# S5 set-up and mixing weights of a hybrid encoder layer: fewer transposes, lag zero by DMA, products by turns over strips, row sums by VectorE

## The chip, the cores and the metric

The kernel runs on one core of one Trainium2 chip. The time is device microseconds of one execution; the median of several executions is what is compared, lower is better.

The names used below: PE is TensorE's matmul side and PEld its weight load, DVE is VectorE, ACT is ScalarE, POOL is GpSimd, SP is the engine that issues most DMAs. PSUM is the memory that TensorE writes and ScalarE and VectorE read.

## The reference, cut to what matters

One layer on 512 positions of width 1024: an input projection, two mixers in parallel, a gated merge, cross-attention to 256 memory rows, and a SwiGLU feed-forward. The change touches the set-up of the two mixers.

```
def s5_scan(u, lam_re, lam_im, log_step, b_re, b_im, c_re, c_im, reverse):
    ...
    lam_bar = jnp.exp(lam * step)
    b_bar = ((lam_bar - 1.0) / lam)[..., None] * b
    bu = jnp.einsum('gpc,lbgc->lbgp', b_bar, u.astype(jnp.complex64))
    _, states = lax.associative_scan(_linear_recurrence, (a, bu), axis=0, reverse=reverse)
    return jnp.einsum('gcp,lbgp->lbgc', c, states).real

def sgu_branch(zu, zv, ln_g, ln_b, w_s, bias):
    zu = jax.nn.gelu(zu)
    zv = layer_norm(jax.nn.gelu(zv), ln_g, ln_b)
    zv = zv.reshape(bsz, seq // CHUNK, CHUNK, SGU_HEADS, SGU_HEAD_DIM)
    sv = jnp.einsum('hts,bnshd->bnthd', w_s, zv) + bias.T[None, None, :, :, None]
    return zu * sv.reshape(bsz, seq, SGU_WIDTH)
```

The S5 mixer has 32 groups of 16 channels with 64 complex states each, and runs in both directions with separate parameters (so every one of b_re, b_im, c_re, c_im has a leading axis of two directions). The gating mixer (SGU) has 8 heads, each with a 128 x 128 matrix over the positions of a chunk of 128.

## The kernel before

**Main stream.** Every large product is done in float32 precision from two parts: a weight block is loaded (`wraw`, three buffers), ScalarE casts its upper part (`whi`, line 85), VectorE subtracts to get the lower part (`wlo`, line 86), and PE adds three products of the parts (`mm3`, line 350). `plan` lists all weight blocks in order; `next_w` begins loads three blocks ahead and splits two blocks ahead. A block of 24 matmuls is a "tick" of about 5 us. The stages in order: projection to zv (first half), to the S5 input u, to zv (second half), to the gates, then the SGU mixing (`psv`), zu, the second gates with w_proj_b, the S5 output's GLU, merge, attention, feed-forward. Products go into five main PSUM banks (`bank`), side work into three (`aux`).

**Side work.** `s5_program` is a generator that hands out VectorE work between ticks; `later(n, f)` traces f n ticks later. What is traced is ordered for each engine by a scheduler that models the times beforehand; the order on each engine is then fixed in the program, and `in_order` keeps an instruction behind what was traced before it on its engine. Each engine and each DMA queue (SP's, POOL's) runs its list in order: an entry that waits holds up all behind it.

**S5 set-up** (`s5_setup`, from line 595). b_re, b_im, c_re and c_im are loaded one after another into one buffer (tag `u`) with the 32 groups on partitions (lines 625 and 630), turned by 16 transposes each (line 634, PSUM tile `pbc`, 32 rows in, 128 states of both directions out) and copied by ScalarE (line 636). VectorE makes powers of the discrete eigenvalues and b_bar.

**Kernel products** (`s5_kernels`, once for each of four octants of 8 groups). For chunks of 8 positions the response at lags -7 to 7 is made as a product: `e` (VectorE: c times powers) against `bd`, which holds b_bar of the two directions side by side in 32 columns. PSUM tile `pk` has four strips of 32 partitions, one for each group of four; `tile_position=(0, 32 * j)` puts the weights into column strip j of the array. A group takes two matmuls of 128 columns (real and imaginary part, line 786) and two of 16 columns (line 789), which add the second direction's lag zero to the first direction's. Each float32 matmul is two records of the profile. All four of a group come one after another, then the next strip's. ScalarE copies the result to `ks` (line 799), VectorE adds the skip d (line 800), POOL's queue writes it to DRAM (`spill`, eight DMAs, lines 807 and 808) and two ticks later loads it back as the Toeplitz block `tt` (`load`, line 815). `s5_outputs` uses tt in `py` (line 894). Octants 0 and 1 are made before the S5 inputs, octants 2 and 3 behind the outputs of octants 0 and 1.

**SGU weights** (`mixing_setup`, traced five ticks into the gate stage). `wsr` holds the eight mixing matrices; PE turns them (`pws`, line 998) and the layer norm's gain and offset (`pgb`, line 1001). With the offset folded out of the einsum, `mix` must hold bias + offset times the row sum of the mixing matrix: two matmuls with a matrix of ones give the row sums on every partition (`prs`, line 1007), and VectorE folds them into `mix`, into which the bias had been loaded at the start (line 1010). `psv` and the operation that adds mix (line 1035) come after the gate stage.

**Others on POOL's queue:** `pow` for the norms' roots (`r`, lines 483 and 984), small memsets, and accumulating DMAs of `plan_sums` (line 268) which add up blocks of later weights in DRAM (`qsum`, `dsum`); each waits for the plain copy that SP issues before it (line 267).

Of the kernel before, what the change touches and what calls it, by code (L numbers as in the profile page):

```python
# [9 lines left out]
F32 = mybir.dt.float32  # L10
F32R = mybir.dt.float32r
AF = mybir.ActivationFunctionType
ALU = mybir.AluOpType
AX = mybir.AxisListType
# [3 lines left out]
P = 128  # L18
# [8 lines left out]
G = 32  # L27
C = 16
GW = 1024
H = 8  # L30
# [9 lines left out]
Q = 8  # L40
# [12 lines left out]
def hybrid_layer_kernel(  # L53
# [8 lines left out]
    nc = tc.nc  # L62
# [17 lines left out]
    def aux(name, shape=(P, 512)):  # L80
        return pa.tile(list(shape), F32, tag="aux", name=name)
# [350 lines left out]
    def later(n, fn):  # L432

        side["later"].append((side["now"] + n, fn))
# [163 lines left out]
    def s5_setup():  # L598
# [19 lines left out]
            lam.append(l)  # L618
        lr, li = lam
        yield 0.3  # L620
        bc = []
        for nm, src in (("br", s5_b_re), ("bi", s5_b_im), ("cr", s5_c_re), ("ci", s5_c_im)):
            if nm[0] == "b":
                row = s5p.tile([G, 2, 64, C], F32, tag="u", name="row" + nm)
                nc.sync.dma_start(row, src[0].rearrange("d g p c -> g d p c"))
                rows = row.rearrange("g d p c -> g (d p) c")
            else:
                row = s5p.tile([G, C, 2, 64], F32, tag="u", name="row" + nm)
                for d in range(2):
                    nc.sync.dma_start(row[:, :, d, :], src[0, d])  # L630
                rows = row.rearrange("g c d p -> g (d p) c")
            ps = aux("pbc", (P, C, G))
            for c in range(C):
                nc.tensor.transpose(ps[:, c, :], rows[:, :, c], ident[:G, :G])
            t = s5p.tile([P, G, C], F32, name="raw_" + nm)
            A_.copy(t, ps.rearrange("p c g -> p g c"))
            bc.append(t)
            yield 0.1
        br, bi, cr, ci = bc
        st["c"] = (cr, ci)  # L640

# [105 lines left out]
    def lc(t, g):  # L747
        return t[:, g].rearrange("p a b -> p (a b)")
# [4 lines left out]
    def s5_kernels(o):  # L753
# [18 lines left out]
        def products():  # L772
            bd = []
            for i in range(2):
                t = s5p.tile([P, GO, 2, C], F32, tag="bd", name="bd", bufs=2)
                nc.gpsimd.memset(t, 0.0)
                for d in range(2):
                    hf = slice(64 * d, 64 * d + 64)
                    nc.scalar.copy(t[hf, :, d, :], st["b"][i][hf, gs, :])
                bd.append(t)  # L780
            ps = aux("pk", (P, 2, P))
            for q in range(2):
                for j in range(4):
                    g = 4 * q + j
                    for i in range(2):
                        nc.tensor.matmul(ps[32 * j:32 * j + 32, q, :], bd[i][:, g].rearrange("p d c -> p (d c)"),  # L786
                                         lc(es[i], g), start=(i == 0), stop=False, tile_position=(0, 32 * j))
                    for i in range(2):
                        nc.tensor.matmul(ps[32 * j:32 * j + C, q, 0:C], bd[i][:, g, 1, :],
                                         es[i][:, g, Q - 1, :], start=False, stop=(i == 1),  # L790
                                         tile_position=(0, 32 * j))
            later(1, lambda: store(ps))

        def store(ps):
# [8 lines left out]
        def spill(ks):  # L803
            kd = dp.tile([GO, C, 15, C], F32, name=f"kd{o}")
            for j in range(4):
                kdj = kd.rearrange("(q j) c l e -> j c q (l e)", j=4)[j]
                nc.gpsimd.dma_start(kdj[:, :, 7 * C:15 * C], ks[32 * j:32 * j + C])
                nc.gpsimd.dma_start(kdj[:, :, 0:7 * C], ks[32 * j + C:32 * j + 2 * C, :, 0:7 * C])
            later(2, lambda: load(kd))

        def load(kd):
# [177 lines left out]
    nc.sync.dma_start(gbr[0:H, :], sgu_ln_g[0].rearrange("(h d) -> h d", d=P))  # L989
    nc.sync.dma_start(gbr[H:2 * H, :], sgu_ln_b[0].rearrange("(h d) -> h d", d=P))  # L990
    mix = np_.tile([P, H, P], F32, tag="gain", name="mix", bufs=2)
    nc.sync.dma_start(mix, sgu_bias[0].rearrange("h t -> (h t)").partition_broadcast(P))

    def mixing_setup():
        for q in range(2):
            ps = aux("pws", (P, 4, P))
            for j in range(4):
                nc.tensor.transpose(ps[:, j, :], wsr[:, 4 * q + j, :], ident)
            nc.scalar.copy(wst[:, 4 * q:4 * q + 4, :], ps)
        ps = aux("pgb", (P, 2 * H))  # L1000
        nc.tensor.transpose(ps, gbr, ident[:2 * H, :2 * H])
        gbc = np_.tile([P, 2 * H], F32, tag="gbc", name="gbc", bufs=1)
        nc.vector.tensor_copy(gbc, ps)

        for q in range(2):
            ps = aux("prs", (P, 4, P))
            nc.tensor.matmul(ps, ones, wst[:, 4 * q:4 * q + 4, :], start=True, stop=True)
            for j in range(4):
                h_ = 4 * q + j
                nc.vector.scalar_tensor_tensor(mix[:, h_, :], ps[:, j, :], gbc[:, H + h_:H + h_ + 1], mix[:, h_, :],  # L1010
                                               ALU.mult, ALU.add)
        return gbc

    gad = dp.tile([KD, P, T], F32, name="gad")
# [4 lines left out]
        nc.sync.dma_start(gad[m - OFF_GA // P], z)  # L1019

    gbcs = []
    later(5, lambda: gbcs.append(mixing_setup()))
    for i in range(NT):
        later(1 + i, lambda i=i: layer_norm(i))
# [652 lines left out]
```

## Time and profile before

| | |
|---|---|
| median of 3 runs | 914.95 us (914.04 to 915.56) |
| span of the profiled execution | 915.4 us |
| PE busy | 900.7 us (98%) |
| DVE busy | 623.8 us (68%) |
| ACT busy | 475.4 us (52%) |
| POOL busy | 102.1 us (11%) |
| granted TensorE clock | 0.998 of full speed |

The span runs from the first to the last instruction of one execution taken by the profiler; the page gives no other time for that execution, so the runs' median stands beside the span. Busy shares are means over the whole span: a stage can be held by an engine that is idle elsewhere. A matmul's duration in the rows is its way through the array and overlaps with the next one's, so the cost of a group of matmuls is read from the distance between starts, or from the start of what follows. "Chain" is the chain of work that ended last, followed back from the last instruction.

### The profile page before, as it was taken

The numbers are of one execution on the slowest core, as the hardware profiler recorded it, in microseconds if no ns is written. First come the engines' busy times: TensorE is split into PE (matmuls) and PEld (weight loads), VectorE is DVE, ScalarE is ACT, GpSimd is POOL, SyncE is SP. The second block draws the span as 40 slices with busy tenths as digits, with TensorE's granted clock in tenths as the row PEclk, the third lists the DMA queues.
The fourth block names the chain that finished last, engine by engine and source line by source line (L and its number), as shares of the span: only waits on it lengthen the run. The fifth ranks groups of instructions, "written<-read, shape, count | busy, mean of one in ns | idle before, by whom it ended". The sixth has DMA issues, their size and how long they took to land.

```text
span 915.4 us, 14510 instructions
## 1 busy us (share of the span) xinstructions
PE 900.7 (98%) x5650; PEld 796.5 (87%) x5650; DVE 623.8 (68%) x1018; ACT 475.4 (52%) x696; POOL 102.1 (11%) x161
## 2 busy tenths in 40 slices
PE   9999999999999999999999999999999999999996
PEld 6888888888888887789899878999999999988885
DVE  5696662888753236858956836776778767899875
ACT  5542985144364334447655634745455454655664
POOL 1004420110025200101000001100020100000000
PEclk9999999999999999999999999999999999999999
DMA  8456574685546577863578416526788873246672
GB/s 252 148 148 185 124 181 141 174 193 149 153 134 146 127 219 206 275 198 120 175 216 252 139 47 184 161 88 149 189 202 212 221 186 93 69 138 200 191 244 90
DMA packets 111974, 153.80 MB, mean 168 GB/s; under 512 B 13521, under 2 KB 78561, under 8 KB 111842
## 3 DMA queue, kind: packets, MB, share of 16 engines
q1 hardware_dynamic: 93026, 128.27, 44.1%
q0 software_dynamic: 16288, 23.57, 15.9%
q10 hardware_dynamic: 2592, 1.05, 0.5%
q8 instruction: 44, 0.72, 0.3%
q14 instruction: 24, 0.20, 0.1%
HBM read 146.08 MB, written 38.24 MB: 201 GB/s over the span
## 4 chain that ended last, share of the span: by engine, by line
PE 90%; ACT 4%; DVE 3%; issue 1%; POOL 0%; DMA 0%; POOLq 0%; SPq 0%; DVEq 0%; ACTq 0%
PE pf L350 27%; PE pt L350 16%; PE px L1273 12%; PE pq L1273 6%; PE dx L350 6%; PE dq L350 3%; PE pv L1273 3%; PE qx L1273 2%; PE dv L350 2%; PE pk L786 2%; PE ptr L506 1%; PE qq L1273 1%; DVE wlo L86 1%; PE po L350 1%; ACT whi L85 1%
## 5 line engine op out<-in xcount | busy, mean ns | idle before, releaser
L86 DVE TENSOR_TENSOR wlo<-wraw,whi 128x1024 fp32r<-128x1024 f32 (+1 forms) x139 | 164.9, 1187 | 109.5 <-ACT whi L85 107.8
L85 ACT CAST whi<-wraw 128x1024 fp32r<-128x1024 f32 (+1 forms) x139 | 142.2, 1024 | 163.0 <-PE pf L350 67.0
L350 PE MATMUL pf<-xn,whi 128*128 128x512 f32 x448 | 140.1, 392 | 0.0
L350 PEld LDWEIGHTS pf<-xn,whi 128*128 128x128 f32 x448 | 83.5, 188 | 17.0 <-issue 0.2
L350 PE MATMUL pf<-xn,wlo 128*128 128x512 f32 x224 | 87.4, 390 | 0.0
L1273 PE MATMUL px<-fn,whi 128*128 128x256 f32 x480 | 86.2, 281 | 0.0
L1273 PEld LDWEIGHTS px<-fn,whi 128*128 128x128 f32 x480 | 73.4, 188 | 0.3 <-ACT u L1532 0.2
L86 DVE TENSOR_TENSOR wlo<-b,whi 128x1024 fp32r<-128x1024 f32 x40 | 48.9, 1222 | 32.8 <-ACT whi L85 32.8
L85 ACT CAST whi<-b 128x1024 fp32r<-128x1024 f32 x40 | 42.0, 1051 | 56.2 <-PE px L1273 28.9
L1273 PE MATMUL px<-fn,wlo 128*128 128x256 f32 x240 | 67.5, 281 | 0.0
L1273 PE MATMUL pq<-s,whi 128*128 128x256 f32 x320 | 57.0, 281 | 0.0
L350 PE MATMUL dx<-whi,s 128*128 128x512 f32 x170 | 53.8, 391 | 1.4 <-ACT whi L85 1.0
L86 DVE TENSOR_TENSOR wlo<-t,whi 128x1024 fp32r<-128x1024 f32 x30 | 36.7, 1224 | 20.9 <-ACT whi L85 20.9
L85 ACT CAST whi<-t 128x1024 fp32r<-128x1024 f32 x30 | 31.5, 1051 | 36.8 <-PE pv L1273 13.3
L350 PEld LDWEIGHTS pf<-xn,wlo 128*128 128x128 f32 x224 | 42.1, 188 | 8.7
L1273 PEld LDWEIGHTS pq<-s,whi 128*128 128x128 f32 x320 | 48.9, 188 | 0.1
L1273 PEld LDWEIGHTS px<-fn,wlo 128*128 128x128 f32 x240 | 46.0, 192 | 0.0
L1273 PE MATMUL pq<-s,wlo 128*128 128x256 f32 x160 | 45.0, 281 | 0.0
L350 PE MATMUL pt<-whi,xn 128*128 128x512 f32 x128 | 42.6, 405 | 0.0
L350 PEld LDWEIGHTS dx<-whi,s 128*128 128x128 f32 x170 | 31.7, 188 | 8.3 <-ACT whi L85 1.2
L350 PE MATMUL dx<-wlo,s 128*128 128x512 f32 x85 | 33.2, 391 | 0.4 <-DVE wlo L86 0.4
L1273 PEld LDWEIGHTS pq<-s,wlo 128*128 128x128 f32 x160 | 30.7, 192 | 0.0
(414 smaller groups left out, 2235.4 us busy)
## 6 DMA issues: line engine op xcount, KB each, us to landing
wraw<-in_w_in_dram SPq DMA_DIRECT2D x36, 512.0 KB, 3.8
dsum<-in_w_down_dram SPq DMA_DIRECT2D x20, 512.0 KB, 6.7
wraw<-dsum SPq DMA_DIRECT2D x20, 512.0 KB, 4.4
b<-in_w_gate_dram SPq DMA_DIRECT2D x15, 512.0 KB, 4.6
b<-in_w_up_dram SPq DMA_DIRECT2D x15, 512.0 KB, 4.6
wraw<-in_w_down_dram SPq DMA_DIRECT2D x15, 512.0 KB, 3.7
dsum<-in_w_down_dram POOLq DMA_DIRECT2D x10, 512.0 KB, 6.8
dsum<-dsum POOLq DMA_DIRECT2D x10, 512.0 KB, 7.4
```

Source lines behind the costliest of these rows:

```text
L85: hi = nc.scalar.copy(dst_hi, src)
L86: lo = nc.vector.tensor_tensor(dst_lo, src, dst_hi.bitcast(F32), ALU.subtract)
L350: nc.tensor.matmul(ps, a[x], b[y], start=start and i == 0, stop=stop and i == 2, skip_group_check=free)
L506: nc.tensor.transpose(ps[:, j, :], src[:, k * P:(k + 1) * P], ident)
L786: nc.tensor.matmul(ps[32 * j:32 * j + 32, q, :], bd[i][:, g].rearrange("p d c -> p (d c)"), lc(es[i], g), start=(i == 0), stop=False, tile ...
L1273: nc.tensor.matmul(ps[:, j, :], a[x], b[y], start=start and j == k == i == 0, stop=k == 3 and i == 2, skip_group_check=True)
```

## The change

It has five parts.

- b is loaded with real and imaginary part on 64 partitions and turned by 16 transposes for both; c is loaded with group and channel on 128 partitions and turned by 8 full transposes. Together 24 in place of 64.
- The two short matmuls of a group, which added the second direction's lag zero, are gone. The spill writes the first direction's part and the second direction's other lags as before, and four more DMAs of POOL's queue add the lag-zero block in DRAM.
- The remaining matmuls of an octant go round the four strips: first the real parts of four groups, then the imaginary parts, and so on. They are kept in program order, and the accumulation flags are set so that the first one of a strip clears it.
- The row sums of the mixing matrices come from one VectorE reduction over `wsr`, one transpose, a store to DRAM and a load that spreads them over all partitions.
- `mixing_setup` scales them by the offset (eight VectorE operations), and a DMA of POOL's queue adds the bias.

```diff
--- before.py
+++ after.py
@@ -618,24 +618,31 @@
             lam.append(l)
         lr, li = lam
         yield 0.3
-        bc = []
-        for nm, src in (("br", s5_b_re), ("bi", s5_b_im), ("cr", s5_c_re), ("ci", s5_c_im)):
-            if nm[0] == "b":
-                row = s5p.tile([G, 2, 64, C], F32, tag="u", name="row" + nm)
-                nc.sync.dma_start(row, src[0].rearrange("d g p c -> g d p c"))
-                rows = row.rearrange("g d p c -> g (d p) c")
-            else:
-                row = s5p.tile([G, C, 2, 64], F32, tag="u", name="row" + nm)
-                for d in range(2):
-                    nc.sync.dma_start(row[:, :, d, :], src[0, d])
-                rows = row.rearrange("g c d p -> g (d p) c")
-            ps = aux("pbc", (P, C, G))
-            for c in range(C):
-                nc.tensor.transpose(ps[:, c, :], rows[:, :, c], ident[:G, :G])
-            t = s5p.tile([P, G, C], F32, name="raw_" + nm)
-            A_.copy(t, ps.rearrange("p c g -> p g c"))
-            bc.append(t)
-            yield 0.1
+        raw_b = s5p.tile([P, 2, G, C], F32, name="raw_b")
+        raw_c = s5p.tile([P, 2, G, C], F32, name="raw_c")
+        brow = s5p.tile([2 * G, 2, 64, C], F32, tag="u", name="brow")
+        for i, src in enumerate((s5_b_re, s5_b_im)):
+            nc.sync.dma_start(brow[i * G:(i + 1) * G], src[0].rearrange("d g p c -> g d p c"))
+        rows = brow.rearrange("g d p c -> g (d p) c")
+        for q in range(2):
+            ps = aux("pbc", (P, C // 2, 2, G))
+            for c in range(C // 2):
+                nc.tensor.transpose(ps[:, c].rearrange("p i g -> p (i g)"), rows[:, :, q * C // 2 + c],
+                                    ident[:2 * G, :2 * G])
+            for i in range(2):
+                A_.copy(raw_b[:, i, :, q * C // 2:(q + 1) * C // 2], ps[:, :, i, :].rearrange("p c g -> p g c"))
+        yield 0.1
+        crow = s5p.tile([P, 2, G * C // P, 2, 64], F32, tag="u", name="crow")
+        for i, src in enumerate((s5_c_re, s5_c_im)):
+            for d in range(2):
+                nc.sync.dma_start(crow[:, i, :, d, :], src[0, d].rearrange("(q g) c p -> (g c) q p", g=P // C))
+        for i in range(2):
+            ps = aux("pbc", (P, G * C // P, P))
+            for q in range(G * C // P):
+                nc.tensor.transpose(ps[:, q, :], crow[:, i, q].rearrange("r d p -> r (d p)"), ident)
+            A_.copy(raw_c[:, i].rearrange("p g c -> p (g c)"), ps.rearrange("p q r -> p (q r)"))
+        yield 0.1
+        bc = [t[:, i] for t in (raw_b, raw_c) for i in range(2)]
         br, bi, cr, ci = bc
         st["c"] = (cr, ci)
 
@@ -780,15 +787,13 @@
                 bd.append(t)
             ps = aux("pk", (P, 2, P))
             for q in range(2):
-                for j in range(4):
-                    g = 4 * q + j
-                    for i in range(2):
-                        nc.tensor.matmul(ps[32 * j:32 * j + 32, q, :], bd[i][:, g].rearrange("p d c -> p (d c)"),
-                                         lc(es[i], g), start=(i == 0), stop=False, tile_position=(0, 32 * j))
-                    for i in range(2):
-                        nc.tensor.matmul(ps[32 * j:32 * j + C, q, 0:C], bd[i][:, g, 1, :],
-                                         es[i][:, g, Q - 1, :], start=False, stop=(i == 1),
-                                         tile_position=(0, 32 * j))
+                for i in range(2):
+                    for j in range(4):
+                        g = 4 * q + j
+                        in_order(nc.tensor.matmul(ps[32 * j:32 * j + 32, q, :],
+                                                  bd[i][:, g].rearrange("p d c -> p (d c)"), lc(es[i], g),
+                                                  start=(i == q == 0), stop=(i == 1), tile_position=(0, 32 * j),
+                                                  skip_group_check=True))
             later(1, lambda: store(ps))
 
         def store(ps):
@@ -806,6 +811,10 @@
                 kdj = kd.rearrange("(q j) c l e -> j c q (l e)", j=4)[j]
                 nc.gpsimd.dma_start(kdj[:, :, 7 * C:15 * C], ks[32 * j:32 * j + C])
                 nc.gpsimd.dma_start(kdj[:, :, 0:7 * C], ks[32 * j + C:32 * j + 2 * C, :, 0:7 * C])
+            for j in range(4):
+                kdj = kd.rearrange("(q j) c l e -> j c q (l e)", j=4)[j]
+                nc.gpsimd.dma_start(kdj[:, :, 7 * C:8 * C], ks[32 * j + C:32 * j + 2 * C, :, 7 * C:8 * C],
+                                    accum_op=ALU.add)
             later(2, lambda: load(kd))
 
         def load(kd):
@@ -989,7 +998,21 @@
     nc.sync.dma_start(gbr[0:H, :], sgu_ln_g[0].rearrange("(h d) -> h d", d=P))
     nc.sync.dma_start(gbr[H:2 * H, :], sgu_ln_b[0].rearrange("(h d) -> h d", d=P))
     mix = np_.tile([P, H, P], F32, tag="gain", name="mix", bufs=2)
-    nc.sync.dma_start(mix, sgu_bias[0].rearrange("h t -> (h t)").partition_broadcast(P))
+    rsd = dp.tile([H, P], F32, name="rsd")
+
+    def row_weights():
+
+        rs = np_.tile([P, 2 * H], F32, tag="gbc", name="rs", bufs=1)[:, 0:H]
+        nc.vector.tensor_reduce(rs, wsr, AX.X, ALU.add)
+        later(0.5, lambda: turn_sums(rs))
+
+    def turn_sums(rs):
+        ps = aux("prs", (H, P))
+        nc.tensor.transpose(ps, rs, ident)
+        rst = np_.tile([H, P], F32, tag="ev", name="rst", bufs=2)
+        nc.vector.tensor_copy(rst, ps)
+        nc.sync.dma_start(rsd, rst)
+        nc.sync.dma_start(mix, rsd.rearrange("h t -> (h t)").partition_broadcast(P))
 
     def mixing_setup():
         for q in range(2):
@@ -1002,13 +1025,10 @@
         gbc = np_.tile([P, 2 * H], F32, tag="gbc", name="gbc", bufs=1)
         nc.vector.tensor_copy(gbc, ps)
 
-        for q in range(2):
-            ps = aux("prs", (P, 4, P))
-            nc.tensor.matmul(ps, ones, wst[:, 4 * q:4 * q + 4, :], start=True, stop=True)
-            for j in range(4):
-                h_ = 4 * q + j
-                nc.vector.scalar_tensor_tensor(mix[:, h_, :], ps[:, j, :], gbc[:, H + h_:H + h_ + 1], mix[:, h_, :],
-                                               ALU.mult, ALU.add)
+        for h_ in range(H):
+            nc.vector.tensor_scalar(mix[:, h_, :], mix[:, h_, :], gbc[:, H + h_:H + h_ + 1], None, ALU.mult)
+        nc.gpsimd.dma_start(mix.rearrange("p h t -> p (h t)"),
+                            sgu_bias[0].rearrange("h t -> (h t)").partition_broadcast(P), accum_op=ALU.add)
         return gbc
 
     gad = dp.tile([KD, P, T], F32, name="gad")
@@ -1019,6 +1039,7 @@
         nc.sync.dma_start(gad[m - OFF_GA // P], z)
 
     gbcs = []
+    row_weights()
     later(5, lambda: gbcs.append(mixing_setup()))
     for i in range(NT):
         later(1 + i, lambda i=i: layer_norm(i))
```

## The prediction

> **What bounds the kernel now.** I read the page first (span, busy shares), then the stages that hold the edited code (busy time by window), then the edited instructions in the chain and the timeline, last the queues that get new work (Pool's, and the DMA landings).
>
> ```profile
> span 915.4 us, 14510 instructions
> ## 1 busy us (share of the span) xinstructions
> PE 900.7 (98%) x5650; PEld 796.5 (87%) x5650; DVE 623.8 (68%) x1018; ACT 475.4 (52%) x696; POOL 102.1 (11%) x161
> ```
>
> TensorE (PE) is busy 98% of the span, so time taken out of its stream comes off the end unless another engine is just behind it. Whether one is, the stages say. Columns of the next rows: stage, length, busy time of PE, PEld, VectorE (DVE), ScalarE (ACT), GpSimd (POOL), then clock, DMA share, GB/s.
>
> ```profile
> 40.00:70.00 30.00, 30.00 (x161) 24.24 (x160) 28.36 (x62) 14.71 (x28) 1.34 (x1) 1.00 0.66 183
> 90.00:140.00 50.00, 49.02 (x290) 42.58 (x289) 30.27 (x41) 45.53 (x74) 15.85 (x22) 1.00 0.65 149
> ```
>
> From 40 to 70 PE never stops, but VectorE is busy 28.36 of 30: 1.64 us of room. From 90 to 140 ScalarE is busy 45.53 of 50 and PE already loses 0.98. In these two stretches a gain could be taken back.
>
> The profiled span, 915.4, is 0.45 above the median of the runs shown (914.95) and inside their spread (914.04 to 915.56): nothing that can be measured lies around the span, and I take savings off 914.95. About 0.2% (1.8 us) is what a measurement of this kernel can tell from no change.
>
> **Part 1: turning b and c.** Pieces of the chain (start, length, what, records); then, in the second fence, the busy time of all pbc transposes in their four windows.
>
> ```profile
> 33.04 1.88 PE pbc L634 x16
> ...
> 51.29 1.11 PE pbc L634 x16
> ...
> 148.85 0.87 PE pws L998 x8
> ...
> 154.65 1.72 PE prs L1007 x4
> ...
> 169.07 3.57 PE psv L1034 x32
> ```
> ```profile
> sum 7.00, PE 6.20; mean PE 1.55
> ```
>
> b is turned in two groups of 16 at 1.88, c in two of 16 at 1.11: 2 x 1.88 + 2 x 1.11 = 5.98 us of PE (the 6.20 also holds the run-out of each group). One transpose of b costs 1.88/16 = 0.118, one of c 0.069; both load 32 x 128 weights, b's from every 16th element, c's without gaps. After the change the two halves of b lie on 64 partitions and 16 transposes do for both, with the same stride and the same 128 columns but twice the rows: I take the same 0.118, so 1.88. c goes as eight full 128 x 128 transposes; that shape is the pws row, 8 in 0.87. New sum 2.75, **saving 3.2**. Bounds for the 64-row form: 0.069 each (saving 4.0) or twice 0.118 (saving 1.4); the stride is unchanged, so it is nearest to 0.118. ScalarE makes six copies out of PSUM for four, with 14.71 of 30 busy there: nothing. SP issues the same six loads; both of b's now go at the start, c's four together right after b's transposes, so c is there earlier than now and the products that need it can only gain: I count nothing.
>
> **Part 2: the kernel products.** Octant 1 in PE's timeline (start, length, instruction, records; one float32 matmul is two records):
>
> ```profile
> 82.12 0.39 PE L350 MATMUL pt<-wlo,xn 128*128 128x512 f32 x1
> 82.44 0.62 PE L786 MATMUL pk<-e,bd 128*32 128x128 f32 x4
> 82.90 0.18 PE L789 MATMUL pk<-e,bd 128*16 128x16 f32 x1
> 82.91 0.30 PE L786 MATMUL pk<-e,bd 128*32 128x128 f32 x1
> 82.93 0.23 PE L789 MATMUL pk<-e,bd 128*16 128x16 f32 x3
> ...
> 86.17 0.26 PE L789 MATMUL pk<-e,bd 128*16 128x16 f32 x4
> 86.36 0.72 PE L350 MATMUL pt<-whi,xn 128*128 128x512 f32 x2
> ```
> ```profile
> sum 26.00, PE 16.09; mean PE 4.02
> ```
>
> The octant holds PE from 82.44 to 86.36: 3.92 us (the second fence sums pk's busy time over all four octants: 16.09, 4.02 each with the run-out). One of its eight groups takes (86.17 - 82.90)/7 = 0.467; one record of 128 columns takes (0.62 - 0.30)/3 = 0.107 from four of them against one; four make 0.427, so the four lag records (L789) cost only 0.04 a group, 0.32 an octant. Entry is 3.92 - 8 x 0.467 = 0.18. The lag matmuls alone are thus worth 4 x 0.32 = 1.3 us. What counts is whether matmuls in different column strips run at once, now that neighbours sit in different strips. The rows say that they can: the first record of the next strip (L786 at 82.91) starts before three lag records of the strip before it (82.93) and runs beside them. Old code has four long records in a row on one strip, so only the lags overlapped. Three sizes follow for an octant's 32 long records:
> - no overlap of long records: 32 x 0.107 + 0.18 = 3.6, saving 0.3 an octant, 1.3 in all;
> - pairs: the two records of a matmul share a strip, so the second waits for the first, and only it runs beside the next matmul's first: 16 x 0.107 + 0.18 = 1.9, saving 2.0, **8.1 in all**;
> - all four strips at once: 8 x 0.107 + 0.18 = 1.0, saving 2.9, 11.5 in all.
>
> I take pairs: the overtaking that the rows show is of one long record by short ones, and four float32 streams at once are seen nowhere.
>
> The Trainium skill ("TensorE: Matmul & The Clock Gate", Part 3: Packing small matmuls) says that matmuls start and end strictly in program order and only weight loads are pulled ahead; by that rule pairs is the most that can come. The three rows at 82.90 to 82.93 disagree with it, since 82.91 stands after all four lag records in the program. The same section gives 2.38 times for three column strips; an estimate from it is 32 x 0.107 / 2.38 + 0.18 = 1.6 us an octant, saving 9.2.
>
> Added behind the products: four accumulating DMAs an octant on Pool's queue, which wait for the eight spills to land, and the loads of tt wait for them.
>
> ```profile
> DMA to landing us min/median/max: 1.7/3.5/8.3
> ```
> ```profile
> 101.47 1.66 POOL L984 TENSOR_TENSOR r<-ms,mhalf 128x1 f32<-128x1 f32 x1
> 107.50 1.52 POOL L984 TENSOR_TENSOR r<-ms,mhalf 128x1 f32<-128x1 f32 x1 [4.38 <-DVE ms L983]
> ...
> 175.81 1.16 POOL L268 DMA_DIRECT2D qsum<-in_w_q_dram  x1 [17.04 <-DMA qsum<-qsum]
> 180.00 1.15 POOL L268 DMA_DIRECT2D qsum<-in_w_q_dram  x1 [3.03 <-DMA qsum<-qsum]
> 186.93 1.15 POOL L268 DMA_DIRECT2D dsum<-in_w_down_dram  x1 [5.78 <-DMA dsum<-in_w_down_dram]
> ...
> 280.97 4.23 POOL L815 DMA_DIRECT2D tt<-kd  x8 [0.56 <-issue]
> ```
> ```profile
> 302.91 0.33 PE L894 MATMUL py<-u,tt 128*128 128x64 f32 x2
> ```
>
> The first fence is the landing of kd's DMAs. Eight issues of tt take 4.23, so four accumulates take 2.1; with 3.5 to land before and 3.5 after, tt comes 9 later. Octant 2's loads, issued by 285.2, are read at 302.91: 17.7 of cover, 8.6 left (without cover all 9 would stand on PE). Octants 0 and 1 are read only behind the scan. What stands behind the wait on Pool is r, the layer norm's root, right after octant 1's spills (101.47, 107.50); ScalarE's scaling waits for r, in the stretch where ScalarE is full. Cost: 0 if r goes ahead of the accumulates, at most 2.1 + 8.3 = 10 if the slowest landing stands ahead of it, of which PE's run-ahead of two split blocks hides most. I take 1.
>
> **Part 3: the row sums.** prs leaves PE: 1.72. One transpose of the sums comes: at the pws rate 0.87/8 = 0.11. **Saving 1.6.** On VectorE (start, length):
>
> ```profile
> 149.98 0.17 DVE L1003 COPY gbc<-pgb 128x16 f32<-128x16 f32 x1
> 155.54 1.12 DVE L1010 SCALAR_TENSOR_TENSOR mix<-prs,gbc,mix 128x128 f32<-128x128 f32 x4 [5.40 <-PE prs L1007]
> ...
> 170.00 0.75 DVE L1035 SCALAR_TENSOR_TENSOR sv<-psv,gbc,mix 128x512 f32<-128x512 f32 x1 [0.41 <-PE psv L1034]
> ```
> ```profile
> qsum<-in_w_q_dram POOLq DMA_DIRECT2D x8, 512.0 KB, 6.9
> ```
>
> Eight fused operations (2 x 1.12 = 2.24) become eight scalings of that size without PSUM (at most 2.24), one reduction of 128 x 1024 (also at most 2.24, eight rows of 128) and a small copy (0.17): up to 2.4 us more on an engine with 20 of 50 us free from 90 to 140. Nothing, unless the reduction is put into the stretch 40 to 70 with its 1.64 of room; then up to 0.6. The bias now comes by an accumulating DMA behind the scalings: 149.98 + 0.17 + 2.24 = 152.4, and 512 KB by Pool land in 6.9: 159.3, needed at 170.00 - 1.6 = 168.4. Cover 9. The sums' store and their broadcast stand on SP, where a wait holds the weight loads behind; three raw buffers are ahead of it. The sums' copy holds one of two ev buffers until its store lands, and ScalarE's squares use that ring. I take 0.5 for both (0 to 2).
>
> **Sum:** 3.2 + 8.1 + 1.6 = 12.9, less 1.5 of waits: 11.4. 914.95 - 11.4 = **903.5**.
>
> **Rivals.**
> - *Four strips at once.* For: 82.91 overtakes. Against: only short records are seen beside a long one. 3.2 + 11.5 + 1.6 - 1.5 = 14.8: 900.1.
> - *Strips take turns without overlap.* For: no two long records overlap anywhere in this trace. Against: the same rows. 3.2 + 1.3 + 1.6 - 1.5 = 4.6: 910.3.
> - *VectorE takes over before 90.* Parts 1 and 2 take 3.2 + 4 = 7.2 off PE before 90 (octants 0 and 1), VectorE's work stays, and it has 1.64 of room in the thickest 30 us. Then up to 5.6 is lost: 909.1. Against: behind 70 it has slack again, and c's earlier arrival lets it start sooner.
> - *The bias lands late* (slower). Pool runs in order and its L268 entries at 175.81, 180.00 and 186.93 wait for DMAs. Put behind the second, the bias lands at 180.00 + 6.9 = 186.9 and sv, now at 170.0, waits 16.9, 18.5 with prs gone. PE goes on through five main banks of psv, 5 x 3.57/4 = 4.5 us, then stands: 14.0 lost, 2.6 more than the 11.4 won: 917.6; behind the third 924.5. It decides from an issue at about 177.4. Against: at the time it becomes ready (152.4) those entries wait for data, and it stands ahead of them in the program.
>
> **How the numbers follow.** Pairs 0.42 (903.5); four strips 0.24 (900.1); no overlap 0.12 (910.3); VectorE 0.09 (909.1); late bias 0.10 (917.6); that the losses just eat the gain 0.03. Faster 0.87, same 0.03, slower 0.10. The range goes from 897.5, four strips with no waits lost (914.95 - 16.3 = 898.7) and b at its better bound, to 912, no overlap with 1.7 more of waits; it leaves the late bias and the even case out.
>
> **What would show it.** pk per octant 1.9 between neighbours on PE (3.6 or 1.0: the rivals); pbc pieces 1.88 + 0.87; prs down to one transpose; on Pool the bias issued before 160 and sv not waiting for it; PE idle from 90 to 140 near 2.5, not 5. Wrong if pk stays above 3, if PE waits for wlo between 40 and 90, or if psv stops halfway.

## The result, and the profile after

The changed kernel takes 911.91 us (907.59 to 915.96 over 20 runs) against 914.81 (912.98 to 915.83 over 20 runs): ratio 0.9968, interval 0.9957 to 0.998. That is faster by 2.9 us where 11.4 were forecast, and the changed kernel's runs lie 8.4 us apart, the old ones 2.9. A run's time is 1.7 to 1.9 us above its span (914.48 and 912.7 for the profiled run of the changed kernel), so the profile of before, with its span of 915.4, belongs to an execution of some 917 us, longer than all 20 runs.

The page of the changed kernel, its first lines:

```profile
span 912.7 us, 14195 instructions
...
PE 885.4 (97%) x5479; PEld 783.3 (86%) x5479; DVE 625.1 (68%) x1020; ACT 474.8 (52%) x698; POOL 114.3 (13%) x178
```

PE's busy time fell by 15.3 us (900.7 before) and the span by 2.7. So the work did go; idle time came in its place. All of it lies ahead of the long run of pt that follows the merge (pt, 72 records, in the chain at 372.25 before, at 370.93 after); behind that point the two kernels differ by 1.4. Busy time up to that point, before and then after:

```profile
0.00:372.25 372.25, 368.24 (x2044) 306.93 (x2045) 228.39 (x527) 184.55 (x271) 66.42 (x121) 1.00 0.64 170
```
```profile
0.00:370.93 370.93, 353.76 (x1873) 294.00 (x1874) 229.30 (x529) 184.08 (x273) 78.81 (x138) 0.97 0.65 172
```

PE is busy 14.5 less (368.24 to 353.76) and idle 13.2 more (4.0 to 17.2).

**The products** fell further than forecast. The 32 records of octant 2 in PE's timeline of the changed kernel, in two pieces, then the busy time of all pk up to 400 us, before and after:

```profile
264.46 0.43 PE L793 MATMUL pk<-e,bd 128*32 128x128 f32 x8
...
267.09 0.86 PE L793 MATMUL pk<-e,bd 128*32 128x128 f32 x24
```
```profile
0.00:400.00 400.00, 16.49 (x256) 14.87 (x256) 1.50 (x4) 1.00 0.65 176
```
```profile
0.00:400.00 400.00, 4.95 (x128) 3.07 (x128) 1.49 (x4) 0.97 0.66 178
```

16.49 to 4.95: 11.5 us, 2.9 an octant. **The turning, the row sums and the bias**, in the timeline of the changed kernel:

```profile
33.57 1.09 PE L630 MATMUL pbc<-ident,brow 64*128 64x64 f32 x8
35.02 1.09 PE L630 MATMUL pbc<-ident,brow 64*128 64x64 f32 x8
43.20 0.60 PE L642 MATMUL pbc<-ident,crow 128*128 128x128 f32 x4
44.33 0.60 PE L642 MATMUL pbc<-ident,crow 128*128 128x128 f32 x4
...
108.14 0.27 PE L1011 MATMUL prs<-ident,rs 128*8 128x128 f32 x1
...
150.76 0.92 POOL L1030 DMA_DIRECT2D mix<-in_sgu_bias_dram  x1 [8.01 <-DVE mix L1029]
...
164.68 0.75 DVE L1056 SCALAR_TENSOR_TENSOR sv<-psv,gbc,mix 128x512 f32<-128x512 f32 x1
```

pbc takes 3.38 (2 x 1.09 + 2 x 0.60) where all of pbc took 6.24; prs is one transpose; the bias is issued at 150.76 and sv waits for nothing.

**Where it was lost.** The chain of the changed kernel around the S5 outputs:

```profile
303.61 17.34 PE pf L350 x76
320.94 0.17 PE py L903 x2
...
326.02 0.24 PE py L905 x2
326.28 0.61 ACT y L910
...
328.29 1.95 DMA yd<-y
...
331.19 3.73 DMA ygt<-yd
334.92 0.63 ACT yg_hi L85
335.60 24.55 PE pf L350 x100
```

py of octant 3 ends at 326.26, and PE's next work, the gate, needs what comes of it: through ScalarE, out to DRAM, back and through a cast. That trip takes 9.3 us and PE stands for all of it. In the kernel before, py of octant 3 is followed by other work. Its chain, then the two rows of PE's timeline where the gate begins (`yb` is the input of another product, `yg` comes of the trip):

```profile
327.40 0.22 PE py L894 x2
...
328.07 17.79 PE pf L350 x78
```
```profile
337.08 0.39 PE L350 MATMUL pf<-yb_hi,wlo 128*128 128x512 f32 x1
337.30 1.07 PE L350 MATMUL pf<-yg_hi,whi 128*128 128x512 f32 x4
```

Of the 78 pf records the first 41, up to 337.30, do not need yg. These 9.2 us covered the trip, which there ended with the cast of yg_hi at 336.5, so the cover was just enough. In the changed kernel the same yb records stand ahead of py. Busy time and granted clock of the changed kernel around the hole (the clock is the third number from the end):

```profile
325.00:330.00 5.00, 1.25 (x12) 1.11 (x10) 0.00 (x0) 0.60 (x1) 0.00 (x0) 0.87 0.50 115
330.00:335.00 5.00, 0.00 (x0) 0.00 (x0) 0.00 (x0) 0.08 (x1) 1.02 (x2) 0.50 0.92 228
335.00:340.00 5.00, 4.41 (x12) 3.54 (x13) 2.59 (x4) 3.44 (x5) 0.00 (x0) 0.60 0.97 304
```

The clock falls to 0.50 in the hole and is still 0.60 in the 5 us behind it. The tt of octant 3 did not come late on the chip. POOL's issues, before and then after:

```profile
308.23 1.12 POOL L815 DMA_DIRECT2D tt<-kd  x2 [7.86 <-PE py L894]
310.04 3.12 POOL L815 DMA_DIRECT2D tt<-kd  x6 [0.69 <-issue]
```
```profile
298.09 3.69 POOL L816 DMA_DIRECT2D kd<-ks  x4
305.56 4.23 POOL L824 DMA_DIRECT2D tt<-kd  x8 [3.78 <-DMA kd<-ks]
```

The last load is issued by 309.8, before by 313.2, although it stands behind four accumulating DMAs (PE itself is 4.8 us earlier here: py of octant 2 starts at 298.30, before at 303.07). PE begins py of octant 3 at 320.94, straight from pf and without a wait. PE's order was fixed beforehand. This gave the theories: **A**, the accumulating DMAs lengthen the way to tt in the scheduler's model of the times, so it puts py of octant 3 behind the last pf that could have covered the trip; **B**, whatever hastens PE ends in this wait, and the DMAs are innocent.

A second hole is PE's wait for zh around 130, 3.2 us long where 1.0 was lost before; a third is at the start, 1.8 for xn.

### The profile page after: what moved, and what is told of

It reads as the page before. It is cut to its first block, busy times and chain, and to the rows that moved or that the text cites. A ratio compares the mean times of both kernels' runs of the same rounds, so it can differ in the third digit from the quotient of the medians.

```text
span 912.7 us, 14195 instructions
## 1 busy us (share of the span) xinstructions
PE 885.4 (97%) x5479; PEld 783.3 (86%) x5479; DVE 625.1 (68%) x1020; ACT 474.8 (52%) x698; POOL 114.3 (13%) x178
## 3 DMA queue, kind: packets, MB, share of 16 engines
q10 hardware_dynamic: 2592, 1.05, 0.5%
## 4 chain that ended last, share of the span: by engine, by line
PE 80%; DVE 2%; DMA 1%; ACT 1%; issue 1%; ACTq 0%; POOL 0%; POOLq 0%; SPq 0%
PE pf L350 25%; PE px L1294 12%; PE pt L350 12%; PE pq L1294 6%; PE dx L350 5%; PE dq L350 3%; PE pv L1294 3%; PE qx L1294 2%; PE dv L350 2%; PE po L350 1%; PE qq L1294 1%; PE ptr L506 1%; PE psc L350 1%; PE psv L1055 1%; PE py L903 1%; PE py L905 1%
## 5 line engine op out<-in xcount | busy, mean ns | idle before, releaser
L350 PEld LDWEIGHTS pt<-whi,xn 128*128 128x128 f32 x128 | 24.8, 196 | 7.8 <-ACT xn L85 2.2
```

The lines of the kernel that those rows point to most:

```text
L350: nc.tensor.matmul(ps, a[x], b[y], start=start and i == 0, stop=stop and i == 2, skip_group_check=free)
```

## The experiments

Every kernel is timed against the kernel before on the same chip, and the ratio is to that. Differences between two changed kernels are differences of medians; where the intervals of their ratios overlap, no difference is shown. Where an expectation counts pf matmuls between py(3) and the gate, that is PE's order as it stands in the program.

**1. Lag zero back in the products (e1_lagmm).** The changed kernel with

```diff
+                for i in range(2):
+                    for j in range(4):
+                        g = 4 * q + j
+                        in_order(nc.tensor.matmul(ps[32 * j:32 * j + C, q, 0:C], bd[i][:, g, 1, :],
+                                                  es[i][:, g, Q - 1, :], start=False, stop=(i == 1), ...))
...
-                nc.gpsimd.dma_start(kdj[:, :, 7 * C:8 * C], ..., accum_op=ALU.add)
```

> The changed kernel, but lag zero of the second direction stays in the products: after the 16 long matmuls of a half octant, eight short ones by turns over the strips, and no accumulating DMAs. Theory A (the accumulating DMAs make octant 3's tt late, so that py of octant 3 stands behind the last pf and PE waits 9.3 us for yg_hi): in PE's program order 30 pf matmuls now stand between py(3) and the gate, 30 x 0.228 = 6.8 us, so of the 9.3 only about 2.5 stay and the dip of the clock with it goes; the short matmuls cost 4 x 0.2 to 0.4 = 0.8 to 1.6 us of PE. 911.9 - 6.8 - 0.7 + 1.2 = about 905.6. Theory B (PE simply arrives earlier at a point that others cannot hasten, the accumulates are innocent): the 9.3 us before yg_hi stay, 912 to 914.

902.97 us, ratio 0.9866 (0.9852 to 0.9881): 8.9 below the changed kernel. PE's longest waits begin with

```profile
PE pf L350 <- ACT yg_hi L85: 2.9, 1, 2.9
```

Theory B falls. The time is 2.6 lower than forecast: the wait for zh (0.5) and the one at the start are smaller here too.

**2. The DMAs alone (e2_accum).** The kernel before, old order of the long matmuls, lag zero by DMA:

```diff
-                    for i in range(2):
-                        nc.tensor.matmul(ps[32 * j:32 * j + C, q, 0:C], bd[i][:, g, 1, :], ...)
...
+                nc.gpsimd.dma_start(kdj[:, :, 7 * C:8 * C], ..., accum_op=ALU.add)
```

> The kernel before, with one part of the change alone: the lag zero matmuls go, the accumulating DMAs come; the order of the long matmuls stays strip by strip. Theory A: PE saves 4 x 0.32 = 1.3 us, but py(3) lands behind the last pf and PE waits 9.3 us or a little less for yg_hi, about 1 more for the clock: 914.8 - 1.3 + 9 = about 922. Theory B (DMAs innocent): 913.5, and PE does not wait for yg_hi.

912.58, ratio 0.9977 (0.9967 to 0.9987): neither number. The wait is there,

```profile
PE pf L350 <- DMA ygt<-yd: 9.1, 1, 9.1
```

but the busy time of pk fell from 16.49 to 5.67, with the matmuls written strip by strip as before:

```profile
0.00:400.00 400.00, 5.67 (x128) 3.79 (x128) 1.48 (x4) 0.98 0.65 177
```

So the short matmuls had cost some 2.7 us an octant, not the 0.32 of the prediction, and the order over the strips was not what made the old products dear (in experiment 9 that order is held fixed).

**3. Products by turns alone (e3_turns).** The kernel before with the loops turned as in the change and the short matmuls behind them as in e1_lagmm.

> The kernel before, with the products alone turned: by turns over the strips, lag zero kept as short matmuls by turns, no accumulating DMAs. Theory A: an octant's products take 1.05 + 0.2 to 0.4 against 3.92, so 4 x 2.5 = 10 us come off PE and come off the end: about 905. Theory B (whatever hastens PE by this much ends in the wait for yg_hi): 912 to 914, with PE waiting 5 us or more there.

901.26, ratio 0.9851 (0.9836 to 0.9866), 14.0 below its kernel before, and yg_hi is not among the waits of PE; pk takes 5.74. Where the expectation reckoned 10 us, 10.75 came from pk. The rest was not fully accounted for: the two profiles differ besides in the start, which differs from one execution to the next (below), and in the waits of PE from 340 to the long pt (0.9 before, none here).

**4. The row sums alone (e5_mix).** The kernel before with `row_weights`, `turn_sums` and the bias by the accumulating DMA.

> The kernel before, with the row sums part alone (reduction on VectorE, one transpose, the trip through DRAM, the bias by an accumulating DMA). If this part is what the prediction took it for: 1.6 off PE, 0.5 back, 913.7. If it causes the two other holes of the changed kernel (the reduction hoisted into the start, where VectorE waits 2.3 us for wsx, about 1.5 us of PE and a lower clock; and PE waiting for ScalarE around 130, where ScalarE waits 2.0 us for a buffer that the sums' store holds, about 2.2 us): 914.8 - 1.6 + 3.7 = about 917.

919.14, ratio 1.0042 (1.0027 to 1.0056): slower by 3.9, though prs left PE, and 2 above the expectation's second case.

**5. Without the row sums (e7_nomix, e9_nomix_accum).** e7 is e3_turns with b and c turned as in the change; e9 is the changed kernel without the row sums part.

> The kernel before with the products by turns (lag zero as short matmuls by turns) and b, c turned by 24 transposes; neither the accumulating DMAs nor the row sums part. Against e3_turns (901.26) this adds the turning alone, against e1_lagmm (902.97) it takes the row sums part out. If the turning is worth its PE time (pbc 6.24 to 3.38 us) and the row sums part costs what e5_mix showed (3.9): 901.26 - 2.9 = 898.4, and 902.97 - 3.9 = 899.1. If the row sums part is worth its 1.6 of PE and e5_mix was dear for another reason: 902.97 + 1.6 = 904.6, and the turning then costs 3 instead of saving 3.

901.6, ratio 0.9861 (0.9843 to 0.988): neither. It lies 1.4 below e1_lagmm and 0.3 above e3_turns, and all three intervals overlap: here neither a cost of the row sums nor a gain of the turning is shown.

> The changed kernel without the row sums part: turning, products by turns and accumulating DMAs are in. If the row sums part costs 3.9 here too: 911.9 - 3.9 = 908, and the wait of PE around 130 (3.2 us for zh) falls back to about 1.0. PE's wait for yg_hi stays at about 9.3 less 7 pf matmuls (1.6) = 7.7, so up to 1.6 more may go: 906.4. If the row sums part is innocent: 911.9 + 1.6 = 913.5.

909.14, ratio 0.994 (0.9924 to 0.9956): 2.8 below the changed kernel; PE waits 8.4 for yg_hi, and zh is not among its longest waits. Against e7_nomix, which differs by the lag zero alone, the DMAs cost 7.5.

**6. Octant 3 alone by matmuls (e10_last).** The changed kernel with the short matmuls and without the accumulating DMAs `if o == 3`.

> The changed kernel, but octant 3 alone has lag zero by short matmuls; octants 0 to 2 keep their accumulating DMAs. In PE's program order 14 pf matmuls now stand between py(3) and the gate (none in the changed kernel, 30 in e1_lagmm), 3.2 us of cover for the 9.3: PE waits about 6 for yg_hi; 911.9 - 3.2 - about 0.5 of clock = about 908. If only octant 3's own DMAs counted and the others were free, it would come to e1_lagmm's 903; if the DMAs were not the cause of the wait, 912.

905.09, ratio 0.9905 (0.9891 to 0.992). PE's wait is the one counted from the order:

```profile
PE pf L350 <- DMA ygt<-yd: 6.0, 1, 6.0
```

The time is 3 us below the expected. Three quarters of what e1_lagmm won (6.8 of 8.9) come from one octant, though the other three keep their DMAs.

**7. The same place without any DMA (e19_late).** e1_lagmm with one number changed:

```diff
-            later(2, lambda: load(kd))
+            later(5 if o == NO - 1 else 2, lambda: load(kd))
```

> e1_lagmm, which has no accumulating DMAs, with one number changed: the loads of octant 3's tt are handed out 5 steps after the spills instead of 2. In PE's program order no pf matmul then stands between py(3) and the gate (30 in e1_lagmm). If the loss of the changed kernel is the place of py(3) in PE's order and nothing in the DMAs themselves: PE waits about 9.3 us for yg_hi, the granted clock falls after it, and the time goes from 903.0 to 909.5 to 911. If it was contention or waiting on the accumulating DMAs: 903 to 904.

909.31, ratio 0.9939 (0.9921 to 0.9957), 6.3 above e1_lagmm, and

```profile
PE pf L350 <- DMA ygt<-yd: 9.2, 1, 9.2
```

There is no accumulating DMA in this kernel. The place of py in PE's order makes the loss; the DMAs only brought it about. The profiles of all 17 kernels agree: with no yb record between py of octant 3 and the gate PE waits 9.1 to 10.1 us (four kernels), with 7 it waits 8.4, with 14 6.0, with 30 1.5 to 2.9 (five kernels), with 37 or more not at all (six). That the scheduler's modelled times are what moves py is inferred; no run reads them.

**8. The turning alone (e4_bc).**

> The kernel before with b and c turned by 24 transposes, nothing else. pbc falls from 6.24 to 3.38 us of PE. If that comes through: 914.8 - 2.9 = 912, at most 1 of it lost since in PE's program order 37 pf matmuls instead of 41 stand between py(3) and the gate (37 x 0.228 = 8.4 us of cover for a trip of 9.3): 912 to 913. If VectorE between 40 and 70 holds the gain back, as the prediction's rival had it: 914 to 915 with new waits of PE for wlo there.

910.65, ratio 0.996 (0.9947 to 0.9973): 4.7 faster by the medians; the interval reaches from 2.5 to 4.9, so it holds the 2.9 of PE that the part saves. No new wait of PE for wlo appears between 40 and 70, where PE is busy 30.00 of 30 with VectorE at 29.68.

**9. What made the old products dear (e14_end, e15_wide).** One run each, so only their traces are used. e14 keeps the strip order and puts a half octant's eight short matmuls behind its eight long ones, all held in that order by `in_order`, which the excerpt does not show; e15 keeps the old loops and takes `bd[i][:, g]` whole in the short ones:

```diff
             for q in range(2):
                 for j in range(4):
                     g = 4 * q + j
                     for i in range(2):
                         nc.tensor.matmul(ps[32 * j:32 * j + 32, q, :], ...)
+                for j in range(4):
+                    g = 4 * q + j
                     for i in range(2):
                         nc.tensor.matmul(ps[32 * j:32 * j + C, q, 0:C], ...)
```

> The kernel before with the products of a half octant in the old order, strip by strip, but all eight short matmuls of lag zero behind the eight long ones instead of two after each strip's two. If what made the old products dear was the alternation of long and short, not the order over the strips: pk falls from 3.92 to about 1.5 us an octant (5.8 in all), as by turns, and the time to about 902. If turns over the strips are needed for records to run at once: pk stays above 3 an octant, 912 to 915.

> The kernel before, old order, but the short matmuls use all 32 columns of a strip's weights instead of 16, which adds terms that the reference does not have to the first direction's lag zero; only the time counts. If the alternation costs by the change of the weights' width: pk falls to 1.4 to 2 us an octant and the time to about 903. If it costs by short and long streams taking turns, or by going back to the same rows of PSUM: pk stays near 3.9 and the time at 915.

905.08 and 913.0. Busy time of pk in e14_end, then in e15_wide:

```profile
0.00:400.00 400.00, 6.89 (x256) 5.62 (x256) 1.50 (x4) 0.99 0.65 179
```
```profile
0.00:400.00 400.00, 16.57 (x256) 15.37 (x256) 1.50 (x4) 1.00 0.64 177
```

The same 128 matmuls (256 records) take 6.89 us where long and short lie apart and 16.49 where they alternate, and the weights' width does not matter. A weight load lasts equally long in both. Here are the loads of the long matmuls in e15_wide, then in e2_accum (durations in ns: least, median, greatest):

```profile
L786 PEld LDWEIGHTS pk<-e,bd x64: 106/109/110, 264.6 to 290.8; 128*32 128x32 f32 x64
```
```profile
L786 PEld LDWEIGHTS pk<-e,bd x64: 106/110/110, 261.5 to 283.4; 128*32 128x32 f32 x64
```

What differs is how many records run at once. In e14_end, with the strip order held:

```profile
264.54 0.44 PE L786 MATMUL pk<-e,bd 128*32 128x128 f32 x8
```

One such record lasts 0.27 to 0.30. In the kernel before, four long ones take 0.62 (the row at 82.44), each 0.107 behind the last; at that pace eight would take 1.05. They take 0.44: the single starts in the trace come in fours, 264.544, 264.551, 264.564 and 264.578, the next four from 264.678 on. Those of e2_accum do so too, while in the kernel before a new long record starts only every 0.11 us (270.517, 270.627, 270.736). The trace does not name a record's strip, but four at a time is what four strips at once look like. So in either order over the strips all four run at once, as soon as short ones no longer stand between one strip's long ones and the next strip's. Whether the short stream or the return to the same strip and rows of PSUM holds the next strip back was not separated.

**10. The reduction held at its place (e8_lagpin, e5_pin, e6_pin, e23_lagmixpin).** In the changed kernel VectorE does the reduction at the start, ahead of layer norm work that PE waits for, and it waits for the matrices to arrive. Its row in the changed kernel, in e1_lagmm and in e5_mix:

```profile
23.33 1.22 DVE L1006 TENSOR_REDUCE rs<-wsx 128x8 f32<-128x1024 f32 x1 [2.32 <-DMA wsx<-in_sgu_w_dram]
```
```profile
22.52 1.22 DVE L1008 TENSOR_REDUCE rs<-wsx 128x8 f32<-128x1024 f32 x1 [0.29 <-DMA wsx<-in_sgu_w_dram]
```
```profile
22.13 1.22 DVE L997 TENSOR_REDUCE rs<-wsx 128x8 f32<-128x1024 f32 x1 [3.82 <-DMA wsx<-in_sgu_w_dram]
```

The edit:

```diff
-        nc.vector.tensor_reduce(rs, wsr, AX.X, ALU.add)
+        in_order(nc.vector.tensor_reduce(rs, wsr, AX.X, ALU.add))
```

> e1_lagmm with the reduction on VectorE held at its place in the program, behind the first layer norms' work, instead of free to be put at 23 us. If the row sums part costs by the reduction that stands at the start, where VectorE waits for wsx and PE then for VectorE and ScalarE: 902.97 less 1.5 to 3, 900 to 901.5. If the start's stalls and dips of the clock come without it, and the cost lies around 130 (the buffer of the sums' copy, the trip through DRAM): 902.5 to 903.5.

901.46, ratio 0.985 (0.9832 to 0.9867), against e1_lagmm's 0.9866 (0.9852 to 0.9881): the intervals overlap, so nothing is decided here, where the wait was only 0.29.

> e5_mix (the row sums part alone, 919.14) with the reduction held at its place in the program, so that VectorE does it at about 97 us instead of waiting for wsx at 22. If the wait at the start is the cost: 2 to 4 us go, 915 to 917, and at the start VectorE's first copy of plam comes at 28 to 30 us instead of 32.3. What may stay is PE's wait for yg_hi (30 pf matmuls behind py(3), 41 before: 1.5 us in e5_mix). If the cost lies around 130, in the sums' trip through DRAM or the buffer that their copy holds: 918.5 to 919.5.

915.72, ratio 1.0007 (0.9997 to 1.0018), 3.4 below e5_mix. VectorE's first copy of plam, e5_mix and then e5_pin:

```profile
32.28 0.19 DVE L617 COPY slab<-plam 128x32 f32<-128x32 f32 x1 [2.05 <-PE plam L615]
```
```profile
27.67 0.19 DVE L617 COPY slab<-plam 128x32 f32<-128x32 f32 x1 [2.07 <-PE plam L615]
```

From 20 to 30 us PE is busy 7.70 of 10 at a granted clock of 0.83 in e5_mix, and 10.00 at 1.00 in e5_pin. So the wait at the start was the row sums part's loss; without it the part comes to nothing, since PE still waits 1.6 for yg_hi and 2.0 for ScalarE around 137.

> The whole changed kernel with the reduction held at its place. py(3) still has no pf matmul behind it, so the wait of about 9.3 for yg_hi stays. If the start's wait for wsx costs 1.5 to 3 and makes the scatter: 909 to 910.5, and runs within 4 us of each other. If not: 911 to 912.5, with the scatter as it was.

910.35, ratio 0.9946 (0.9929 to 0.9964): 1.6 below the changed kernel, as the first case had it, but the intervals overlap, so the gain is not shown. The wait for yg_hi is 10.1. Its runs still lie between 906.74 and 914.33. The scatter does not come from the reduction.

> e3_turns (901.26) with the row sums part added, its reduction held at its place; b and c are turned as before. If, without the wait at the start, the part is worth its PE time: 901.26 - 1.6 = 899.7. If it gives that back by the place of py(3) (30 pf matmuls behind it instead of 48, a wait of 2.2 to 2.9 for yg_hi as in e8_lagpin and e1_lagmm): 901.5 to 902.5.

904.24, ratio 0.9892 (0.9872 to 0.9912): a miss, worse than e3_turns. PE waits 1.8 for yg_hi, as the second case had it; where the rest of the 3 us went was not found (the profiled run, at 907.0, had the later of the two starts described below). In no pair of kernels did the row sums part show a gain.

**The best version.** e3_turns (901.26), e8_lagpin (901.46) and e7_nomix (901.6) cannot be told apart, and e1_lagmm's interval overlaps theirs. Each of the three is about 1.4% faster than the kernel before and 1.1% than the changed one; e3_turns is the smallest edit.

## Why the prediction was wrong

The sign held, the size did not: 11.4 forecast, 2.9 measured. Point by point.

- **The step that failed: the cover of the accumulating DMAs.** The sum gave all waits 1.5 us; PE's idle time grew by 13.2. The prediction found tt 9 us later, gave octant 2 a cover of 17.7, put octants 0 and 1 behind the scan, and went on without octant 3. Its py is the last thing ahead of a trip of 9.3 us that PE must wait for, and the 9.2 us of yb records behind it were the only cover. It also read all cover off the old order, as if the order would stay. On the chip tt was there in time (issued by 309.8, read at 320.94), but py had been put behind the last pf that could cover. The price is 7.5 us (e7_nomix against e9_nomix_accum) to 8.9 (e1_lagmm against the changed kernel); e19_late shows it without the DMAs. None of the rivals had this mechanism. That 911.91 comes close to the forecast's slow end of 912 and to the rivals at 909.1 and 910.3 speaks for none of them: those stand for products without overlap or for VectorE taking over, and pk is at 4.95 and PE never stops from 40 to 70.
- **The products: right sign, mis-sized.** 8.1 was forecast for pairs of strips, 11.5 came, and the mechanism is that of the rival of four strips at once (the eight long records in 0.44 us). The prediction set that rival lower because four streams were seen nowhere, which held for the old trace alone. What it had wrong besides is what kept the strips apart. It was not the order over them: e2_accum, written strip by strip, has pk at 5.67, the changed kernel by turns at 4.95, so turns are worth 0.7 in all. It was the short matmuls between them, priced at 0.04 a group by subtracting four times 0.107, the pace of one strip alone, from 0.467. The Trainium skill ("TensorE: Matmul & The Clock Gate", Part 3: Packing small matmuls) gives 2.38 times for three column strips. The trace, with four strips, shows more: thirty records in the 1.11 us of e2_accum are 0.037 each against 0.107, 2.9 times. The upper end of pairs that the prediction drew from that section's rule of order did not hold; and in e14_end, where 16 long records stand ahead of the 16 short ones in the program, the first short ones start at 264.79 while long ones still start at 264.90.
- **The turning: right.** 3.2 forecast, 2.9 measured on PE (6.24 to 3.38), split 2.18 and 1.20 in place of 1.88 and 0.87; alone it made the kernel faster by 4.7 (2.5 to 4.9). VectorE did not take over between 40 and 70.
- **The row sums: wrong sign.** 1.6 less 0.5 was forecast; alone the part cost 3.9. The prediction named the case that the reduction is put into a full stretch and looked at 40 to 70. It went to 23, ahead of the data it needs. The wait that the prediction saw at the ev buffer came: in the changed kernel ScalarE waited 1.96 for the sums' store at 114, against 0.5 taken for both waits; what of it reached PE was not separated.
- **Bias: right.** Issued at 150.76, forecast 152.4, and sv does not wait; the slower rival fell.
- **POOL's wait, 1 us:** r was not held by the accumulating DMAs; it follows them by 8.42 us, waiting for VectorE (113.13 in POOL's timeline). PE's longer wait for zh around 130 was not settled: 3.2 in the changed kernel, 2.0 in e6_pin, 1.0 in e10_last, 0.5 in e1_lagmm.
- **The span.** The prediction took it that nothing measurable lies around the span. Each run's time is 1.7 to 1.9 above it. The savings were taken off the median, so the sum does not change.
- **What would show it** served: PE idle from 90 to 140 was 3.7, above the 2.5 named, and pk, 1.24 an octant, was nearest to the 1.0 of four strips. It had no line for the stretch from 300 to 340, where most was lost.

Open, besides: whether the turning keeps its gain on top of e3_turns, why the short matmuls hold the next strip back, and what makes the changed kernel's runs scatter over 8 us.

## What to carry to other kernels

A step moved onto a queue is not priced by the latency it adds alone: ask for every consumer, the last one above all, which work stands behind it on the bound engine, and whether a reordering scheduler will keep it there. Before an overlap is put down to a new order, take the suspected instructions apart on the chip: here the strips ran at once in either order as soon as the short matmuls no longer stood between them, and the smallest edit, which leaves lag zero in the products, was worth 14 us. An instruction that may be moved freely can be moved ahead of its data; hold it in place where the engine has work that others wait for.

## What the runs showed of the hardware

- Four column strips can run at once without turns, as starts in fours show (the trace does not name the strip): eight long records of 0.27 to 0.30 us take 0.44 in e14_end. Two short matmuls behind each strip's two long ones undo it: in the kernel before four long records take 0.62, and all pk 16.49 us in place of 6.89. The weights' width changes nothing (16.57), and a weight load of a long matmul lasts 0.106 to 0.110 in all these kernels.
- In a hole of 9.3 us the granted clock was 0.50, and 0.60 in the 5 us in which PE took up its work again. The Trainium skill ("TensorE: Matmul & The Clock Gate", Part 1: The HAM clock gate) says that an idle window halves the clock until PE has been busy for a window; the trace agrees. Shorter waits showed it too: behind e1_lagmm's 2.9 us the clock was 0.50 from 324.2 to 327.5, behind e23_lagmixpin's 1.8 us from 327.7 to 331.0. Behind e5_pin's 1.6 us it stayed at 1.00.
- The start has two courses. Two kernels with the same PE program there, the one before and then e3_turns:

```profile
5.63 3.78 PE L558 MATMUL pg<-g_row,ones 1*128 1x512 f32 x4
```
```profile
5.27 1.98 PE L558 MATMUL pg<-g_row,ones 1*128 1x512 f32 x4
```

The four matmuls take 3.78 or 1.98 us, and VectorE's first copy of plam comes at 30.19 or at 27.84. The windows give the later one a granted clock of 1.00 over the first 20 us and the earlier one 0.91, but the clock column cannot tell them apart: the trace's first clock record stands at 13.6 us in the first and at 4.8 in the second, and what lies ahead of it counts as full. Five of the 17 profiles have the later start: before, e1_lagmm, e7_nomix, e19_late and e23_lagmixpin. So up to 2.4 us of any difference between two single profiles can be this.
